# One-hot tiles with tokens in pairs: a gate matmul whose columns lie four bytes apart instead of thirty-two

## The chip, the cores and the metric

The kernel runs on one core of one Trainium2 chip. Its time is the device time of one execution in microseconds (us); three runs of the kernel before are given below. Where a part is read more closely, the numbers come from one profiled execution of it.

## The reference, cut to what matters

The program is two transformer blocks on 512 tokens of width 1024, in float32. The first block ends in a layer of product-key experts. Eight heads each choose 16 of 128 x 128 = 16384 experts for a token; an expert is a pair of rows, one of `u_tab` and one of `v_tab`, and a number `e1 * 128 + e2`.

```python
def peer(h, wq, subkeys, u_tab, v_tab):
    q = (ht @ wq).reshape(T, PEER_HEADS, 2, PEER_HALF)
    sc = jnp.einsum('thpd,hpnd->thpn', q, subkeys)
    v1, i1 = lax.top_k(sc[:, :, 0], PEER_TOPK)
    v2, i2 = lax.top_k(sc[:, :, 1], PEER_TOPK)
    ...
    best, pos = lax.top_k(cand, PEER_TOPK)
    e1 = jnp.take_along_axis(i1, pos // PEER_TOPK, axis=-1)
    e2 = jnp.take_along_axis(i2, pos % PEER_TOPK, axis=-1)
    experts = (e1 * PEER_KEYS + e2).reshape(T, PEER_HEADS * PEER_TOPK)
    gates = jax.nn.softmax(best, axis=-1).reshape(T, PEER_HEADS * PEER_TOPK)

    def block(args):
        xb, eb, gb = args
        u = jnp.take(u_tab, eb, axis=0)
        vv = jnp.take(v_tab, eb, axis=0)
        act = jax.nn.gelu(jnp.einsum('tkd,td->tk', u, xb), approximate=False)
        return jnp.einsum('tk,tkd->td', gb * act, vv)
```

## The kernel before, in words

For 448 of the 512 tokens (`ND`) the kernel does not gather expert rows. It computes the first product for all 16384 experts, 128 chunks of 128 experts (`expert_up`), takes the gelu, multiplies each value by the token's gate for that expert (zero for most), and multiplies with the second table. So it needs the gates as a dense matrix: for each token a 128 x 128 table, rows `e1`, columns `e2`. The other 64 tokens are gathered later.

The gate matrix is made in the loop `for b in range(NB)` (lines 769 to 791), 28 blocks of 16 tokens (`TB`). The partitions are the 128 choices of a token (head and rank); `e1T`, `e2T` hold the two expert halves of each choice as float16, one column a token, and `ghi`, `glo` its gate as a sum of two float16 numbers. In each block VectorE (DVE) makes four tiles of 128 x 2048 float16 numbers:

- `oa` (line 779): 1 where the index of `iot` equals `e1T`, else 0, for all 128 indices and 16 tokens; `ob` (line 780) the same for `e2T`;
- `oh` and `ol` (lines 781, 782): `ob` times `ghi`, and times `glo`.

Then TensorE multiplies, for each token, `oa` (the weights) with `oh` (line 787) and adds the product with `ol` (line 788): 32 gate matmuls a block, 128 columns each, and a weight load for each. Four tokens share a PSUM tile `gps`, which ScalarE (ACT) scales and copies to `gst` (line 789); at the end of a block `gst` is stored to DRAM as `gdr[b]` from ScalarE's queue (line 790). The tiles are laid out as `[partition, index, token]` with the 16 tokens last, so the 128 columns that one matmul reads lie 16 elements, 32 bytes, apart, for the weights as for the moving operand.

Between the blocks, `expert_up` with `on_pool=2` (line 791) spreads 22 chunks of the first expert product. A chunk is 24 matmuls of 448 columns (`part3`, lines 175, 178, 179): the weights come as float32 (`raw`, loaded from SyncE's queue) and are split by `load_w` in a rounded part `wh` (line 159) and a rest `wl` (line 162), both on GpSimd (POOL) in this stage; ScalarE takes the gelu (line 612). Outside this stage `wh` is made by ScalarE (line 161), and `wl` by VectorE or GpSimd.

The engines have queues of their own and wait for each other by semaphores; the order in each queue comes from the tile framework's scheduler. On TensorE a burst of 32 gate matmuls alternates with a chunk of 24, and at six places two bursts follow each other. `oa`, `oh` and `ol` have three buffers, `ob` one, `gst` two, `wh` and `wl` four, `raw` three, and PSUM gives eight banks to `gps` and the chunks together. After the stage come eight more chunks, and the load of `gt` from `gdr` (line 854) for the second expert product. Everything else (attention and mixer before it; experts' second product, differential attention, two feed-forward layers and a short convolution after it) isn't touched.

Of the kernel before, what the change touches and what calls it, by code (L numbers as in the profile page):

```python
# [23 lines left out]
P = 128  # L24
# [59 lines left out]
def decoder_kernel(ctx: ExitStack, tc: tile.TileContext, I, out):  # L84
# [59 lines left out]
    def after(inst, first):  # L144
        """inst is to follow first on their engine"""
        if first is not None:
            tc.add_manual_dep(inst.ins, first.ins.name, mybir.DependencyInfo(
                mybir.DependencyClass.NoSync, mybir.DependencyReason.DATA), reason="pace")
# [3 lines left out]
    def load_w(src, n=8, on_pool=0, pool=wp):  # L152
        """the two parts of a weight tile; on_pool: how many of them GpSimd makes"""
        raw = wp.tile([P, 8, P], F32, tag="raw", name="raw", bufs=3)
        wh = pool.tile([P, 8, P], F32R, tag="wh", name="wh", bufs=4)
        wl = pool.tile([P, 8, P], F32R, tag="wl", name="wl", bufs=4)
        nc.sync.dma_start(raw[:, :n], src)
        if on_pool > 1:
            G.tensor_copy(wh[:, :n], raw[:, :n])
        else:  # L160
            A.activation(wh[:, :n], raw[:, :n], AF.Copy)  # L161
        (G if on_pool else V).tensor_tensor(wl[:, :n], raw[:, :n], wh[:, :n].bitcast(F32), ALU.subtract)  # L162
        return wh, wl
# [17 lines left out]
    def linear(srcs, evac, xh=None, xl=None, N=T, n=8, on_pool=0, head=None, tail=None, between=None,  # L181
               ws=None):
        """evac(j, ps, c0, c1) takes columns c0:c1 of product j. head: column ranges of the first four products,
        done contraction step by contraction step; tail: (ranges, then) of the last four."""
        xh = xh or (lambda i: hi[:, i])
        xl = xl or (lambda i: lo[:, i])
        order = list(range(n))
        j0, j1 = 0, len(srcs)
        if head:
            j0 = len(ws or srcs[:4])  # L190
            ws = ws or [load_w(src, n, on_pool) for src in srcs[:4]]
            for c0, c1 in head:
                pss = [lin_tile()[:, :c1 - c0] for _ in ws]
                for i in order:
                    for w, ps in zip(ws, pss):
                        part3(ps, w, xh, xl, i, c0, c1, i == order[0], i == order[-1])
                    if between:
                        between(i)
                    if i >= DEFER and held and next(held[0], held) is held:
                        held.pop()  # L200
                for j, ps in enumerate(pss):
                    evac(j, ps, c0, c1)
        if tail:
            j1 -= 4
        for j in range(j0, j1):
            w = load_w(srcs[j], n, on_pool)
            ps = lin_tile()[:, :N]
            for i in order:
                part3(ps, w, xh, xl, i, 0, N, i == order[0], i == order[-1])
            evac(j, ps, 0, N)  # L210
        if tail:
            ranges, then, *pool = tail
            ws = [load_w(src, n, on_pool, *pool) for src in srcs[j1:]]
            steps = iter(())
            for c0, c1 in ranges:
                for j, w in enumerate(ws):
                    ps = lin_tile()[:, :c1 - c0]
                    for i in order:
                        part3(ps, w, xh, xl, i, c0, c1, i == order[0], i == order[-1])
                    evac(j1 + j, ps, c0, c1)  # L220
                    if j >= TDEFER:
                        next(steps, None)
                list(steps)
                steps = then(c0, c1)
            held.append(steps)
# [23 lines left out]
    def head_rstd(dst, rows, nt):  # L249
        """dst [P, nt, 16]: rstd of 64-wide heads from their rows of summed squares [16, nt * P]."""  # L250
        rw = scr.tile([P, T], F32, tag="s2k", name="rw")
# [15 lines left out]
    def head_rows(dst, r, nt):  # L267
        """dst [16, nt * P]: the rows of r [P, nt, 16]."""
        pt = ax_tile("pt")
        for t in range(nt):  # L270
            PE.transpose(pt[:16, t * P:(t + 1) * P], r[:, t], ident)
        A.activation(dst[:16, :nt * P], pt[:16, :nt * P], AF.Copy)
# [31 lines left out]
    def rstd_cols(a, c0, c1):  # L304
        """[P, 4]: rstd of each token (a column per 128 of them) from per-partition partial sums a."""
        n, nt = c1 - c0, (c1 - c0) // P
# [7 lines left out]
    def spread(r, n):  # L314
        """PSUM [P, n]: the columns of r on every partition."""
        nt = n // P
# [5 lines left out]
    def norm_apply(xt, c0, c1, a, acol, shcol, oh, ol):  # L322
        """in steps: the sums over the channels, then some channels at a time"""
        r = rstd_cols(a, c0, c1)
# [26 lines left out]

# [1 line left out]
    ws = []  # L353
# [9 lines left out]
    with tc.tile_pool(name="mix", bufs=1) as mx:  # L363
# [41 lines left out]
        def window(g):  # L405
            """the mean over the last 2 << g tokens, less the token itself"""
            cur = pch[:, g]
# [144 lines left out]
    def mod_tile(l, j, pool, cs, junk, tag):  # L552
        """columns of modulation vector tile j of layer l: ada_w products with silu(c), along the free dimension"""
        aw = pool.tile([P, D], F32, tag=tag, name="aw", bufs=3)
# [13 lines left out]
    def mod_work(pool, tiles):  # L568
        """gives step(k): runs k more of the listed (layer, tile) products; a callable in the list runs in its place"""
        cs = pool.tile([P, 1, D], F32, name="csw")  # L570
# [17 lines left out]

# [1 line left out]
    gdr = drp.tile([NB, P, P, TB], F32, name="gdr")  # L590
# [17 lines left out]
    def expert_up(c0, c1, on_pool=0):  # L608
        """gelu of the first expert product of chunks c0:c1: to DRAM below NSP, else to the end of acts"""
        def ev_u(c, ps, *_):  # L610
# [10 lines left out]
    rt = rtc.__enter__()  # L621
    iot = rt.tile([P, P, TB], F16, name="iot")
    e1T = rt.tile([P, T], F16, name="e1T")
# [5 lines left out]
    with tc.tile_pool(name="rs", bufs=1) as rs:  # L629
# [26 lines left out]
        if NG:  # L656
            for q in range(2):
# [8 lines left out]
                A.activation(h2n[:, q * T:(q + 1) * T], pn, AF.Copy)  # L666
        G.iota(iot, [[1, P], [0, TB]], base=0, channel_multiplier=0, allow_small_or_imprecise_dtypes=True)
        expert_up(0, NPRE, 1)

        # candidate pairs (a, b) of the two sorted lists that can be among the best 16: (a + 1)(b + 1) <= 16  # L670
        tvv = tv.rearrange("p t (h s) k -> p (t h) s k", s=2)
# [14 lines left out]

        # gates
        bmax = rs.tile([P, NT, 8, 1], F32, name="bmax")
# [9 lines left out]

        # expert halves of the chosen pairs
        SH = [P, NT, 16, 8]  # L700
# [68 lines left out]
    with tc.tile_pool(name="gb", bufs=2) as gb:  # L769
        for b in range(NB):  # L770
            bs = slice(b * TB, (b + 1) * TB)

            def bc(tl):
                return tl[:, bs].unsqueeze(1).to_broadcast([P, P, TB])
            oa = gb.tile([P, P, TB], F16, tag="oa", name="oa", bufs=3)
            ob = gb.tile([P, P, TB], F16, tag="ob", name="ob", bufs=1)
            oh = gb.tile([P, P, TB], F16, tag="oh", name="oh", bufs=3)
            ol = gb.tile([P, P, TB], F16, tag="ol", name="ol", bufs=3)
            V.tensor_tensor(oa, iot, bc(e1T), ALU.is_equal)
            V.tensor_tensor(ob, iot, bc(e2T), ALU.is_equal)  # L780
            V.tensor_tensor(oh, ob, bc(ghi), ALU.mult)
            V.tensor_tensor(ol, ob, bc(glo), ALU.mult)
            gst = gb.tile([P, P, TB], F32, tag="gst", name="gst")
            for t0 in range(0, TB, 4):
                ps = ax_tile("gps").rearrange("p (u n) -> p u n", u=4)
                for u in range(4):
                    PE.matmul(ps[:, u], oa[:, :, t0 + u], oh[:, :, t0 + u], start=True, stop=False)  # L787
                    last_g = PE.matmul(ps[:, u], oa[:, :, t0 + u], ol[:, :, t0 + u], start=False, stop=True)  # L788
                A.activation(gst[:, :, t0:t0 + 4].rearrange("p i t -> p t i"), ps, AF.Copy, scale=1.0 / GS)  # L789
# [7 lines left out]
    with tc.tile_pool(name="ev", bufs=1) as ev_:  # L797
# [35 lines left out]

        # row gathers and modulation, spread over the groups that also run the first expert product
        work = []
# [55 lines left out]

# [1 line left out]
    with tc.tile_pool(name="da", bufs=1) as da:  # L893
# [132 lines left out]
        with tc.tile_pool(name="at", bufs=4) as at:  # L1026
# [7 lines left out]
            def attn_out(h, aT, th):  # L1034
                """steps of the output of head h for token tiles 2 * th, 2 * th + 1"""
                W = 2 * P
# [154 lines left out]

# [1 line left out]
    mod_tiles = [(1, j) for j in range(24, 40)] + [lambda: mods_done(1, 24, 40, ((3, mod[:, 1, 32:40], "n2_1"),))]  # L1193
# [131 lines left out]
```

## Time and profile before

| | |
|---|---|
| time, median of 3 runs | 3267.92 us (3258.57, 3267.92, 3268.86) |
| span of the profiled execution, first to last instruction | 3261.2 us |
| its own time | not recorded beside the span |
| TensorE busy, share of the span | 3148.2 us, 97% |
| VectorE / ScalarE / GpSimd busy | 1846.0 / 1108.5 / 499.9 us |
| mean granted TensorE clock | 0.956 |
| one-hot operations (lines 779 to 782) | 112, median 1.22 us each |
| gate matmuls (lines 787, 788) | 896, from 401.8 us on, the last starts at 750.5 us |

How to read it: times are counted from the first instruction. A matmul's record holds its way through the array, so records of neighbours overlap; what a matmul costs is the distance from start to start. "PEclk" is the share of full clock that TensorE was granted. In a row of the list of waits stand who waited, for whom, the total in us, how often, and the longest. In a row of the timeline stand the start, the duration, the engine, the line, the operation, output and inputs.

### The profile page before, as it was taken

How to read it: one execution, taken by the hardware profiler on the slowest of the kernel's cores; microseconds unless marked ns; L12 is line 12 of the kernel's file. 1: busy time of each engine (PE TensorE's matmuls, PEld its weight loads, DVE VectorE, ACT ScalarE, POOL GpSimd, SP SyncE). 2: the span in 40 equal slices, each digit the busy share in tenths (PEclk: the TensorE clock that was granted, in tenths of full speed). 3: DMA queues.
4: the chain of work that ended last, by engine and by line, in shares of the span. 5: the costliest groups of instructions: out<-in, count | busy, mean ns of one | idle time of the engine just before them, and what ended most of it. 6: DMA issues, size and time to landing. Idle time of an engine off the chain costs nothing.

```text
span 3261.2 us, 38749 instructions
## 1 busy us (share of the span) xinstructions
PE 3148.2 (97%) x15100; PEld 2618.5 (80%) x15100; DVE 1846.0 (57%) x3378; ACT 1108.5 (34%) x1611; POOL 499.9 (15%) x438
## 2 busy tenths in 40 slices
PE   8999799999999999999999999999999999999999
PEld 6688677778899888888888877655888888898887
DVE  6678943422775666666666574287654446653333
ACT  4433233334233232232232353276422233332221
POOL 1133422113000222222222020000000000000000
PEclk9999877679999999999999999999999999999999
DMA  4222333336775776666666332000364434533332
GB/s 141 65 73 92 115 125 138 120 133 216 230 238 154 234 237 227 221 230 222 227 227 221 120 129 68 26 1 27 102 203 142 130 116 130 161 129 92 91 101 78
DMA packets 132071, 467.24 MB, mean 143 GB/s; under 512 B 14896, under 2 KB 25312, under 8 KB 127920
## 3 DMA queue, kind: packets, MB, share of 16 engines
q1 hardware_dynamic: 79200, 269.56, 26.3%
q0 software_dynamic: 42752, 156.59, 14.6%
q10 hardware_dynamic: 9936, 38.63, 3.0%
q8 instruction: 118, 1.93, 0.3%
q14 instruction: 65, 0.53, 0.0%
HBM read 419.86 MB, written 40.63 MB: 141 GB/s over the span
## 4 chain that ended last, share of the span: by engine, by line
PE 59%; issue 18%; DMA 11%; DVE 8%; POOL 2%; ACT 2%; POOLq 0%; DVEq 0%; ACTq 0%
PE mm L175 14%; PE mm L179 14%; PE mm L178 14%; DMA gu<-in_peer_ur,idx 4%; DMA gu<-in_peer_vr,idx 4%; PE gps L787 3%; PE gps L788 3%; PE sp L1086 2%; PE po L1044 1%; DMA aw<-in_ada_w 1%; DMA gt<-gdr 1%; DVE wl L162 1%; POOL gu L820 1%; PE mm L1010 1%; PE mm L1012 1%
## 5 line engine op out<-in xcount | busy, mean ns | idle before, releaser
L179 PE MATMUL mm<-hi,wl 128*128 128x512 f32 (+2 forms) x2496 | 930.7, 373 | 41.9 <-DVE wl L162 39.9
L175 PE MATMUL mm<-hi,wh 128*128 128x512 f32 (+2 forms) x2496 | 937.9, 376 | 13.3 <-ACT wh L161 8.2
L161 ACT ACTIVATE wh<-raw 128x1024 fp32r<-128x1024 f32 (+1 forms) x468 | 491.4, 1052 | 1338.4 <-PE mm L178 871.9
L178 PE MATMUL mm<-lo,wh 128*128 128x512 f32 (+2 forms) x2496 | 928.9, 372 | 0.0
L162 DVE TENSOR_TENSOR wl<-raw,wh 128x1024 fp32r<-128x1024 f32 (+1 forms) x425 | 515.0, 1214 | 281.6 <-ACT wh L161 275.7
L179 PEld LDWEIGHTS mm<-hi,wl 128*128 128x128 f32 x2496 | 483.5, 194 | 117.2 <-DVE wl L162 49.6
L175 PEld LDWEIGHTS mm<-hi,wh 128*128 128x128 f32 x2496 | 485.8, 195 | 84.1 <-ACT wh L161 11.3
L178 PEld LDWEIGHTS mm<-lo,wh 128*128 128x128 f32 x2496 | 484.6, 194 | 64.1 <-issue 0.8
L178 PE MATMUL mm<-pl,wh 128*128 128x448 f32 (+3 forms) x1436 | 523.4, 364 | 5.1 <-DVE pl L871 5.1
L179 PE MATMUL mm<-ph,wl 128*128 128x448 f32 (+3 forms) x1436 | 523.3, 364 | 0.8 <-DVE wl L162 0.8
L175 PE MATMUL mm<-ph,wh 128*128 128x448 f32 (+3 forms) x1436 | 523.3, 364 | 0.5 <-ACT ph L870 0.5
L178 PEld LDWEIGHTS mm<-pl,wh 128*128 128x128 f32 x1436 | 270.5, 188 | 33.8 <-DVE pl L871 5.8
L179 PEld LDWEIGHTS mm<-ph,wl 128*128 128x128 f32 x1436 | 270.6, 188 | 30.1 <-DVE wl L162 1.9
L175 PEld LDWEIGHTS mm<-ph,wh 128*128 128x128 f32 x1436 | 270.5, 188 | 29.0 <-ACT ph L870 0.9
L162 POOL TENSOR_TENSOR wl<-raw,wh 128x1024 fp32r<-128x1024 f32 x65 | 159.3, 2455 | 225.1 <-ACT wh L161 201.5
L787 PE MATMUL gps<-oh,oa 128*128 128x128 f16 x448 | 188.8, 423 | 0.0
L788 PE MATMUL gps<-ol,oa 128*128 128x128 f16 x448 | 188.0, 422 | 0.0
L789 ACT ACTIVATE gst<-gps 128x512 f32<-128x512 f32 x112 | 122.1, 1092 | 106.4 <-PE gps L788 104.9
L866 DVE TENSOR_TENSOR act<-act,gt 128x448 f32<-128x448 f32 x128 | 79.8, 634 | 104.1 <-DMA gt<-gdr 98.6
L347 DVE SCALAR_TENSOR_TENSOR x<-mm,mod,x 128x512 f32<-128x512 f32 (+1 forms) x76 | 50.5, 666 | 148.4 <-PE mm L179 148.2
L555 POOL DMA_DIRECT2D aw<-in_ada_w x96 | 52.3, 546 | 519.1 <-DVE mod L556 330.9
L870 ACT ACTIVATE ph<-act 128x448 fp32r<-128x448 f32 x128 | 72.7, 576 | 151.3 <-DVE act L866 150.8
(350 smaller groups left out, 3341.6 us busy)
## 6 DMA issues: line engine op xcount, KB each, us to landing
raw<-in_peer_u SPq DMA_DIRECT2D x128, 512.0 KB, 4.0
raw<-in_peer_v SPq DMA_DIRECT2D x128, 512.0 KB, 3.7
aw<-in_ada_w POOLq DMA_DIRECT2D x96, 512.0 KB, 5.0
raw<-in_w_gu SPq DMA_DIRECT2D x88, 512.0 KB, 3.7
gdr<-gst ACTq DMA_DIRECT2D x28, 1024.0 KB, 3.9
gt<-gdr POOLq DMA_DIRECT2D x16, 1792.0 KB, 11.7
raw<-in_w_dn SPq DMA_DIRECT2D x32, 448.0 KB, 3.4
raw<-in_sc_in SPq DMA_DIRECT2D x24, 512.0 KB, 3.7
```

The source lines that it names most:

```text
L161: A.activation(wh[:, :n], raw[:, :n], AF.Copy)
L162: (G if on_pool else V).tensor_tensor(wl[:, :n], raw[:, :n], wh[:, :n].bitcast(F32), ALU.subtract)
L175: mm = PE.matmul(ps, wh[:, i], xh(i)[:, c0:c1], start=first, stop=False)
L178: PE.matmul(ps, wh[:, i], xl(i)[:, c0:c1], start=False, stop=False)
L179: PE.matmul(ps, wl[:, i], xh(i)[:, c0:c1], start=False, stop=last)
L555: nc.gpsimd.dma_start(aw, I["ada_w"][l, j])
L787: PE.matmul(ps[:, u], oa[:, :, t0 + u], oh[:, :, t0 + u], start=True, stop=False)
L788: last_g = PE.matmul(ps[:, u], oa[:, :, t0 + u], ol[:, :, t0 + u], start=False, stop=True)
L789: A.activation(gst[:, :, t0:t0 + 4].rearrange("p i t -> p t i"), ps, AF.Copy, scale=1.0 / GS)
L866: V.tensor_tensor(at.rearrange("p (b t) -> p b t", t=TB), at.rearrange("p (b t) -> p b t", t=TB), gt[:, :, c], ALU.mult)
L870: A.activation(ph, at, AF.Copy)
L1086: PE.matmul(sps[e][:, c0:c1], q2[pr, qi, ts], k2[pr, qi, c0:c1], start=True, stop=True)
```

## The change

The tiles `oa`, `ob`, `oh` and `ol` become `[partition, token pair, index, token of the pair]`: 8 pairs, 128 indices, 2 tokens. The columns of one matmul then lie 2 elements, four bytes, apart. `iot` holds each index twice instead of 16 times and is read again for each pair (a step of 0); the vectors `e1T`, `e2T`, `ghi`, `glo` are read two tokens at a time, and each two are repeated over the 128 indices. Sizes of the tiles, count of operations and of matmuls, and the numbers computed are the same. (The diff also drops comments, left out here.)

```diff
-    iot = rt.tile([P, P, TB], F16, name="iot")
+    iot = rt.tile([P, P, 2], F16, name="iot")
...
-        G.iota(iot, [[1, P], [0, TB]], base=0, channel_multiplier=0, allow_small_or_imprecise_dtypes=True)
+        G.iota(iot, [[1, P], [0, 2]], base=0, channel_multiplier=0, allow_small_or_imprecise_dtypes=True)
...
+            PAIRS = [P, TB // 2, P, 2]
+
             def bc(tl):
-                return tl[:, bs].unsqueeze(1).to_broadcast([P, P, TB])
-            oa = gb.tile([P, P, TB], F16, tag="oa", name="oa", bufs=3)
-            ob = gb.tile([P, P, TB], F16, tag="ob", name="ob", bufs=1)
-            oh = gb.tile([P, P, TB], F16, tag="oh", name="oh", bufs=3)
-            ol = gb.tile([P, P, TB], F16, tag="ol", name="ol", bufs=3)
-            V.tensor_tensor(oa, iot, bc(e1T), ALU.is_equal)
-            V.tensor_tensor(ob, iot, bc(e2T), ALU.is_equal)
+                return tl[:, bs].rearrange("p (a u) -> p a u", u=2).unsqueeze(2).to_broadcast(PAIRS)
+            oa = gb.tile(PAIRS, F16, tag="oa", name="oa", bufs=3)
+            ob = gb.tile(PAIRS, F16, tag="ob", name="ob", bufs=1)
+            oh = gb.tile(PAIRS, F16, tag="oh", name="oh", bufs=3)
+            ol = gb.tile(PAIRS, F16, tag="ol", name="ol", bufs=3)
+            io = iot.unsqueeze(1).to_broadcast(PAIRS)
+            V.tensor_tensor(oa, io, bc(e1T), ALU.is_equal)
+            V.tensor_tensor(ob, io, bc(e2T), ALU.is_equal)
             V.tensor_tensor(oh, ob, bc(ghi), ALU.mult)
             V.tensor_tensor(ol, ob, bc(glo), ALU.mult)
...
                 for u in range(4):
-                    PE.matmul(ps[:, u], oa[:, :, t0 + u], oh[:, :, t0 + u], start=True, stop=False)
-                    last_g = PE.matmul(ps[:, u], oa[:, :, t0 + u], ol[:, :, t0 + u], start=False, stop=True)
+                    at = (slice(None), (t0 + u) // 2, slice(None), u % 2)
+                    PE.matmul(ps[:, u], oa[at], oh[at], start=True, stop=False)
+                    last_g = PE.matmul(ps[:, u], oa[at], ol[at], start=False, stop=True)
```

On TensorE, VectorE, ScalarE and SyncE the instructions stand in the same order as before, row for row. On GpSimd one instruction has another size, the index pattern of line 667, made before the expert layer's first product:

```order
 L247 TENSOR_TENSOR r_1336<-rp,mhalf 128x2
 L602 DMA fold<-in_fold 128x64
-L667 IOTA iot 128x2048
+L667 IOTA iot 128x256
 L631 DMA skT<-in_subkeys 128x2048
 L247 TENSOR_TENSOR r_1551<-rp,mhalf 128x2
```

Nothing moved there; `iot` is written with 256 elements a partition in place of 2048.

## The prediction

> **What bounds the kernel now.** I read the page first: its span, the two rows of section 2 for TensorE, and the groups of the gate matmuls.
>
> ```profile
> span 3261.2 us, 38749 instructions
> PE   8999799999999999999999999999999999999999
> PEclk9999877679999999999999999999999999999999
> L787 PE MATMUL gps<-oh,oa 128*128 128x128 f16 x448 | 188.8, 423 | 0.0
> L788 PE MATMUL gps<-ol,oa 128*128 128x128 f16 x448 | 188.0, 422 | 0.0
> L789 ACT ACTIVATE gst<-gps 128x512 f32<-128x512 f32 x112 | 122.1, 1092 | 106.4 <-PE gps L788 104.9
> ```
>
> TensorE is busy from end to end, so what it saves shows at the end unless another engine is late. Its clock is low in slices 5 to 9, and the gate matmuls run there. The table of windows gives that stage from the first gate matmul to the last, the stretch after it, and then the gate matmuls alone (the last two rows) in a stretch at full clock and one at half clock.
>
> ```profile
> core 0: us, PE busy (x) PEld busy (x) DVE busy (x) ACT busy (x) POOL busy (x), PEclk, DMA share, GB/s
> 401.76:750.53 348.77, 348.77 (x1402) 253.04 (x1401) 130.36 (x107) 133.07 (x133) 69.91 (x39) 0.71 0.34 126
> 769.00:810.00 41.00, 40.33 (x195) 35.98 (x194) 18.35 (x23) 19.39 (x25) 12.13 (x9) 1.00 0.81 267
> ...
> core 0: us, PE busy (x), PEclk, DMA share, GB/s
> 452.90:456.40 3.50, 3.50 (x15) 1.00 0.17 61
> 456.60:467.90 11.30, 11.30 (x49) 0.50 0.38 139
> ```
>
> In the stage TensorE never stops; VectorE (DVE), ScalarE (ACT) and GpSimd (POOL) are busy for 130, 133 and 70 us of 349. The list of waits says on whom they wait:
>
> ```profile
> POOL wh L159 <- PE mm L178: 222.5, 18, 19.0
> DVE oh L781 <- PE gps L787: 105.0, 12, 9.3
> ACT gst L789 <- PE gps L788: 104.0, 108, 2.3
> DVE oa L779 <- PE gps L788: 74.4, 12, 8.8
> ```
>
> All of them wait for TensorE. The important reading is in the last two window rows: a gate matmul takes 3.50 / 15 = 0.233 us at full clock and 11.30 / 49 = 0.231 us at half clock. What costs the same at both clocks isn't limited by the array; what is left is the reading of the two operands, whose 128 columns lie 32 bytes apart. The 896 matmuls at 0.235 us (a burst of 32 from 438.81 to 446.34 us) are 211 us of the stage. The other 138 us are 21 chunks of the first expert product, 504 matmuls of 448 columns, 0.274 us each on average. The timeline shows why these too are slow:
>
> ```profile
> 434.32 0.57 PE L175 MATMUL mm<-hi,wh 128*128 128x448 f32 x1
> 434.69 0.57 PE L178 MATMUL mm<-lo,wh 128*128 128x448 f32 x1
> ...
> 436.34 0.36 PE L175 MATMUL mm<-hi,wh 128*128 128x448 f32 x1
> 436.54 0.37 PE L178 MATMUL mm<-lo,wh 128*128 128x448 f32 x1
> ...
> 438.81 0.45 PE L787 MATMUL gps<-oh,oa 128*128 128x128 f16 x1
> ...
> 446.34 0.74 PE L175 MATMUL mm<-hi,wh 128*128 128x448 f32 x1
> ```
>
> After a gate burst they start 0.37 us apart (half clock), some 4 us later 0.20 us apart. So a gate burst, busy by the record, doesn't hold the clock up.
>
> **What the change costs and saves.** No instruction is added, removed or moved on TensorE, VectorE, ScalarE or SyncE. GpSimd's index pattern becomes an eighth as large; it is made at 174 us, long before its first use at 393 us, and counts as nothing. What changes is how long the 896 gate matmuls (with their weight loads) and the 112 one-hot operations take.
>
> *Gate matmul at a step of four bytes.* No row has two-byte columns at this step, so I bound it. Below: 448-column matmuls at full clock, whose four-byte columns also lie four bytes apart, start 0.20 us apart, so 128 columns are 0.058 us. Above: 128-column matmuls in plain float32, each with weights of its own:
>
> ```profile
> 283.86 1.16 PE L649 MATMUL pss<-skT,qt 128*128 128x128 f32 x8
> 284.86 0.27 PE L665 MATMUL pn<-ident,tmp 128*128 128x128 f32 x1
> ```
>
> Eight in 1.00 us are 0.125 us each. I take 0.07, near the lower end: the step is that of the 448-column rows, and plain float32 costs twice as much a column there. TensorE then needs 896 x 0.07 = 63 us, and 504 x 0.203 = 102 us for the expert chunks if the clock stays up: 165 us instead of 349. Alone, it would finish at 402 + 165 = 567 us.
>
> [...]
>
> *What is late next.* VectorE and GpSimd. Their timelines where both are busy, and GpSimd alone:
>
> ```profile
> 393.30 1.23 DVE L779 TENSOR_TENSOR oa<-iot,e1T 128x2048 f16<-128x2048 f16 x1
> 394.44 1.22 DVE L780 TENSOR_TENSOR ob<-iot,e2T 128x2048 f16<-128x2048 f16 x1
> ...
> 396.72 1.22 DVE L781 TENSOR_TENSOR oh<-ob,ghi 128x2048 f16<-128x2048 f16 x1
> 397.85 2.06 DVE L782 TENSOR_TENSOR ol<-ob,glo 128x2048 f16<-128x2048 f16 x1
> 399.84 3.42 DVE L779 TENSOR_TENSOR oa<-iot,e1T 128x2048 f16<-128x2048 f16 x1
> 403.17 2.06 DVE L780 TENSOR_TENSOR ob<-iot,e2T 128x2048 f16<-128x2048 f16 x1
> ...
> 469.56 1.22 DVE L780 TENSOR_TENSOR ob<-iot,e2T 128x2048 f16<-128x2048 f16 x1
> 470.82 1.23 DVE L781 TENSOR_TENSOR oh<-ob,ghi 128x2048 f16<-128x2048 f16 x1
> ...
> 398.92 3.25 POOL L162 TENSOR_TENSOR wl<-raw,wh 128x1024 fp32r<-128x1024 f32 x1
> 402.12 2.04 POOL L159 CAST wh<-raw 128x1024 fp32r<-128x1024 f32 x1
> 473.98 1.04 POOL L159 CAST wh<-raw 128x1024 fp32r<-128x1024 f32 x1 [17.64 <-PE mm L178]
> 475.10 2.38 POOL L162 TENSOR_TENSOR wl<-raw,wh 128x1024 fp32r<-128x1024 f32 x1
> ```
>
> A one-hot operation alone takes 1.14 us from start to start (393.30 to 394.44). The one that starts at 399.84 while GpSimd subtracts until 402.17 takes 3.42 us: it waits until GpSimd is done and then needs its 1.1 us. GpSimd's 2.38 us become 3.25 in the same way. The two engines take turns, so their times add. Today that is hidden, as both idle most of the stage. From 393.3 us on there are 112 VectorE operations, 28 x (4 x 1.14 + 0.12) = 131 us (0.12: where `oh` directly follows the `ob` that it reads, it starts 470.82 - 469.56 = 1.26 us after it, not 1.14), and 20 chunks on GpSimd at 1.04 + 2.38 = 3.42 us, 68 us. Together 199 us: the last operands are ready at 592 us, later than TensorE's 567, so this pair ends the stage. The last 32 gate matmuls take 2 us more: 595 us instead of 750.5, 155 us less. Where the pair stands still for a moment, or TensorE falls to half clock while it waits for operands, some of that is lost; I allow 8 us (one 0.3 us gap for each block), which leaves **147 us**.
>
> ScalarE needs its 133 us and stays under 199. The stage's 44 MB (349 us at 126 GB/s) in 193 us would be 228 GB/s, less than the 267 of the stretch at 769 us. What follows (eight more chunks, then the load of the gates from DRAM) hangs on the end of the stage in the same order and moves with it; the clock comes back there some us sooner, which I don't count.
>
> *One-hot operations in the new layout.* All of their operands still have neighbouring elements last, but the gate and index vectors now come in runs of two elements instead of sixteen. The shortest runs that the trace has at two bytes are eight:
>
> ```profile
> 372.06 0.42 DVE L734 TENSOR_TENSOR prd<-msk,li 128x512 f16<-128x512 f16 x1
> 372.39 0.29 DVE L729 TENSOR_SCALAR msk<-bb 128x512 f16<-128x512 f16 x1
> ```
>
> 512 elements take 0.33 us from start to start and 2048 take 1.14, so the 1536 more cost 0.81 us: 0.53 ns an element, with runs of eight as with runs of sixteen, and some 0.06 us are fixed. So I take 1.14 us unchanged. Bounds: no gain below, since no two-byte row of this engine with two operands is quicker per element; above, half that rate, as if the two elements of a run were handled one by one: 2048 x 1.06 ns + 0.06 = 2.2 us.
>
> [...] No run here shows runs of two.
>
> **Sum.** The page is one execution with a span of 3261.2 us; the three runs are 3258.57, 3267.92 and 3268.86 us, so some 7 us lie around the span, or the execution was a quicker one. Against the median: 3268 - 147 = **3121 us**. A difference under 0.3% (10 us, the spread of those runs) can't be told from none.
>
> **Rivals.**
> - *TensorE stays the bound (0.17).* Either a gate matmul costs 0.125 us, 112 + 102 = 214 us, the stage ends at 616, 134 us less: 3134 us. (The pair is overtaken from (592 - 402 - 102) / 896 = 0.098 us on.) Or the clock doesn't come back: 504 x 0.373 + 896 x 0.107 (0.373 x 128 / 448) = 284 us, end at 686, 3203 us. For it: half clock follows each burst today. Against it: denser matmuls elsewhere hold 1.00. [...]
> - *VectorE falls to half its rate (0.10).* 28 x (4 x 2.20 + 0.12) + 68 = 318 us, end at 711 + 2, 37 us less: 3231 us. For it: no row has such short runs. Against it: runs of eight cost nothing over sixteen.
> - *The gate matmul doesn't get faster (0.04).* If any gap between columns, not the 32 bytes, costs 0.235 us, nothing changes: 3268 us. Four-byte columns at the same step speak against it.
> - *Slower (0.03).* If each run of two costs VectorE three steps, where it now costs one of 1.06 ns (two elements at 0.53), an operation is 1024 x 3 x 1.06 = 3.2 us + 0.06, the pair needs 28 x 13.2 + 68 = 438 us, and the stage ends at 833: 83 us more, 3351 us. This decides from (750 - 2 - 393 - 68) / 112 = 2.56 us an operation on.
>
> **Numbers.** The forecast has 0.66. Its own range is 3102 (the pair overlaps a little, as from 396.72 to 408.48 us where 12.5 us of work took 11.8, and the later matmuls find a full clock) to 3140. With the first half of the first rival the range goes to 3162. Faster by over 0.3%: 0.66 + 0.17 + 0.10 = 0.93; same 0.04; slower 0.03.
>
> **What would show it.** Gate matmuls start 0.06 to 0.1 us apart. The stage takes 190 to 205 us. VectorE has next to no idle time in it, and its operations still have a least time of 1.22 us with more of them stretched to 2 to 3.4. TensorE now waits for `ol` or `oh` from VectorE, for the first time. The clock of the stage rises over 0.9. The windows from the stage's end on look as before. I am wrong if the gate matmuls stay above 0.1 us, the one-hot operations get longer when nothing contends, or VectorE idles while TensorE waits.

## The result

The changed kernel takes 3111.19 us (median of 4 runs, 3109.35 to 3115.48), the kernel before 3266.22 us in the same comparison. The ratio is 0.9532, with a 95% interval from 0.9517 to 0.9547: 155 us, 4.7%, less. In the page of the kernel after, the span and the two rows of TensorE:

```profile
span 3109.8 us, 38748 instructions
PE   8899788899999999999999999999999999999999
PEclk9999889999999999999999999999999999999999
```

Of the dip of the clock in slices 5 to 9, two slices at 8 tenths are left. The table of windows shows the gate stage, from its first gate matmul to the last, and then one burst of 32 gate matmuls alone (columns as in the prediction):

```profile
402.04:595.46 193.42, 166.57 (x1401) 153.20 (x1401) 181.32 (x107) 114.46 (x131) 91.78 (x39) 0.93 0.62 223
...
478.00:485.00 7.00, 2.01 (x32) 1.00 0.46 184
```

The stage takes 193.4 us where it took 348.8; that is 155.4 us less, all of the 155 us between the medians. TensorE now is busy for 167 us of it, VectorE for 181. The burst alone lasts from 480.78 to 482.60, 0.057 us a gate matmul instead of 0.235. Behind a long wait it is slower:

```profile
480.78 0.23 PE L792 MATMUL gps<-oh,oa 128*128 128x128 f16 x1
...
482.60 0.45 PE L175 MATMUL mm<-hi,wh 128*128 128x448 f32 x1
...
570.63 0.29 PE L792 MATMUL gps<-oh,oa 128*128 128x128 f16 x1 [4.48 <-DVE oa L783]
571.76 0.27 PE L793 MATMUL gps<-ol,oa 128*128 128x128 f16 x1 [0.84 <-DVE ol L786]
571.83 0.31 PE L792 MATMUL gps<-oh,oa 128*128 128x128 f16 x1
571.93 0.31 PE L793 MATMUL gps<-ol,oa 128*128 128x128 f16 x1
572.04 0.31 PE L792 MATMUL gps<-oh,oa 128*128 128x128 f16 x1
```

From 571.83 to 574.92 us the granted clock is 0.50, and the matmuls start 0.107 us apart. Five of the 28 bursts are of this kind, wholly or in part, each behind a wait of 3.1 to 4.9 us: some 114 of the 896 gate matmuls. The list of waits of this stage has turned round:

```profile
POOL wh L159 <- PE mm L178: 73.0, 18, 11.7
PE gps L792 <- DVE oa L783: 9.7, 3, 4.5
PE gps L793 <- DVE ol L786: 8.8, 8, 3.1
PE gps L792 <- DVE oh L785: 8.4, 2, 4.9
DVE oa L783 <- PE gps L793: 0.5, 1, 0.5
```

Before, VectorE waited 179 us for gate matmuls. Now it waits 0.5 us, and TensorE waits 27 us for VectorE (all three tiles). What VectorE and GpSimd (POOL) do in the middle of the stage, and how the stage ends, is in the timeline:

```profile
426.01 3.32 DVE L785 TENSOR_TENSOR oh<-ob,ghi 128x2048 f16<-128x2048 f16 x1
429.26 1.21 DVE L786 TENSOR_TENSOR ol<-ob,glo 128x2048 f16<-128x2048 f16 x1
430.51 2.11 DVE L784 TENSOR_TENSOR ob<-iot,e2T 128x2048 f16<-128x2048 f16 x1
432.65 3.27 DVE L785 TENSOR_TENSOR oh<-ob,ghi 128x2048 f16<-128x2048 f16 x1
435.84 1.21 DVE L786 TENSOR_TENSOR ol<-ob,glo 128x2048 f16<-128x2048 f16 x1
...
430.50 1.04 POOL L159 CAST wh<-raw 128x1024 fp32r<-128x1024 f32 x1 [2.24 <-PE mm L178]
431.62 3.23 POOL L162 TENSOR_TENSOR wl<-raw,wh 128x1024 fp32r<-128x1024 f32 x1
...
584.88 1.22 DVE L786 TENSOR_TENSOR ol<-ob,glo 128x2048 f16<-128x2048 f16 x1
...
593.65 0.23 PE L792 MATMUL gps<-oh,oa 128*128 128x128 f16 x1
```

An `ob` that meets GpSimd's rounding, and an `oh` that meets its subtraction, take 2.1 and 3.3 us instead of 1.2, and GpSimd's own subtraction takes 3.2 instead of 2.4: they take turns. VectorE works through from 393.6 to 586.1 us. The last burst starts only at 593.65, since TensorE is then behind: GpSimd has finished its last chunk of the stage at 568 us, and from there VectorE is quicker (4.86 us a block) than TensorE with a burst and a chunk (1.82 + 4.89). The burst at half clock before these blocks adds 1.5 us to that.

### The profile page after: what moved, and what is told of

Same layout as the page of the kernel before. It is cut to its first block, busy times and chain, and to the rows that moved or that the text cites. A ratio compares the mean times of both kernels' runs of the same rounds, so it can differ in the third digit from the quotient of the medians.

```text
span 3109.8 us, 38748 instructions
## 1 busy us (share of the span) xinstructions
PE 2969.9 (96%) x15100; PEld 2519.1 (81%) x15100; DVE 1897.2 (61%) x3378; ACT 1091.9 (35%) x1611; POOL 521.0 (17%) x438
## 4 chain that ended last, share of the span: by engine, by line
PE 52%; issue 18%; DVE 14%; DMA 11%; POOL 3%; ACT 2%; DVEq 0%; POOLq 0%; ACTq 0%; SPq 0%
PE mm L179 14%; PE mm L175 14%; PE mm L178 13%; DMA gu<-in_peer_ur,idx 4%; DMA gu<-in_peer_vr,idx 4%; PE sp L1091 2%; DVE ob L784 2%; DVE oh L785 1%; DMA aw<-in_ada_w 1%; PE po L1049 1%; DVE ol L786 1%; DVE oa L783 1%; DMA gt<-gdr 1%; DVE wl L162 1%; PE mm L1015 1%
## 5 line engine op out<-in xcount | busy, mean ns | idle before, releaser
L179 PE MATMUL mm<-hi,wl 128*128 128x512 f32 (+2 forms) x2496 | 918.4, 368 | 40.0 <-DVE wl L162 37.1
L175 PE MATMUL mm<-hi,wh 128*128 128x512 f32 (+2 forms) x2496 | 922.1, 370 | 13.3 <-ACT wh L161 8.1
L178 PE MATMUL mm<-lo,wh 128*128 128x512 f32 (+2 forms) x2496 | 916.0, 367 | 0.0
L179 PEld LDWEIGHTS mm<-hi,wl 128*128 128x128 f32 x2496 | 474.5, 190 | 112.9 <-DVE wl L162 46.0
L175 PEld LDWEIGHTS mm<-hi,wh 128*128 128x128 f32 x2496 | 475.6, 191 | 80.1 <-ACT wh L161 11.2
L178 PEld LDWEIGHTS mm<-lo,wh 128*128 128x128 f32 x2496 | 475.5, 191 | 62.4 <-issue 0.8
L162 POOL TENSOR_TENSOR wl<-raw,wh 128x1024 fp32r<-128x1024 f32 x65 | 174.0, 2679 | 196.4 <-ACT wh L161 172.9
L829 DVE CUSTOM_DVE_ANT_0 gjk<-gu,h2n 128x1024 f16<-128x1024 f32 x64 | 78.3, 1223 | 71.4 <-DMA gu<-in_peer_ur,idx 71.1
L345 DVE TENSOR_TENSOR x<-x,mm 128x448 f32<-128x448 f32 (+2 forms) x132 | 80.2, 608 | 67.1 <-PE mm L179 66.9
L794 ACT ACTIVATE gst<-gps 128x512 f32<-128x512 f32 x112 | 106.1, 1105 | 28.6 <-PE gps L793 25.8
```

The source lines that it names most:

```text
L175: mm = PE.matmul(ps, wh[:, i], xh(i)[:, c0:c1], start=first, stop=False)
L178: PE.matmul(ps, wh[:, i], xl(i)[:, c0:c1], start=False, stop=False)
L179: PE.matmul(ps, wl[:, i], xh(i)[:, c0:c1], start=False, stop=last)
L345: V.tensor_tensor(x[:, j, c0:c1], x[:, j, c0:c1], ps, ALU.add)
L829: dve_gated(V.tensor_tensor_reduce(gjk, gu, h2n, 1.0, 0.0, ALU.mult, ALU.add, dot[:, s:s + 1]))
```

## The experiments

**Which operand, and which distance.** The layouts were varied by two numbers, `GA` for the weights `oa` and `GM` for `ob`, `oh` and `ol`: so many tokens lie side by side, and the columns are twice as many bytes apart. The changed kernel is `GA = GM = 2`, the one before 16.

```diff
-            PAIRS = [P, TB // 2, P, 2]
+            GA, GM = 2, 16        # w4_m32; 16, 2: w32_m4; 4, 4: step8; 8, 8: step16; 1, 1: step2
+            def sh(g):
+                return [P, TB // g, P, g]
...
-                    at = (slice(None), (t0 + u) // 2, slice(None), u % 2)
+                    wa, ma = ((slice(None), (t0 + u) // g, slice(None), (t0 + u) % g) for g in (GA, GM))
-                    PE.matmul(ps[:, u], oa[at], oh[at], start=True, stop=False)
+                    PE.matmul(ps[:, u], oa[wa], oh[ma], start=True, stop=False)
```

*Weights 4 bytes apart, moving operand 32:*

> Weights in pairs (4 bytes apart), moving operand as before (32 bytes apart). Theory A, the moving operand's read sets the 0.235 us: a gate matmul stays at 0.23 us from start to start and the time stays near 3266 us. Theory B, the weights' read sets it: 0.06 to 0.1 us and about 3111 us. Theory C, each of the two reads alone takes 0.23 us, side by side: 0.23 us here and in the opposite mix too. Theory D, the two reads follow each other and half of the cost is each one's: about 0.14 us here and there, stage 896 x 0.14 + 504 x 0.21 = 231 us, time about 3150 us.

*Weights 32 bytes apart, moving operand 4:*

> Weights as before (32 bytes apart), moving operand in pairs (4 bytes apart). Theory A (moving operand): 0.06 to 0.12 us a gate matmul, time about 3111 to 3135 us. Theory B (weights): 0.23 us and 3266 us. Theory C (each alone): 0.23 us and 3266 us. Theory D (half each): 0.14 us and about 3150 us.

Timeline and weight loads (least, median and longest time in ns) of the first, then of the second:

```profile
479.77 0.41 PE L796 MATMUL gps<-oh,oa 128*128 128x128 f16 x1
480.00 0.41 PE L797 MATMUL gps<-ol,oa 128*128 128x128 f16 x1
480.24 0.41 PE L796 MATMUL gps<-oh,oa 128*128 128x128 f16 x1
...
L796 PEld LDWEIGHTS <-oa x448: 96/128/152, 404.2 to 741.2; 128*128 128x128 f16 x150
```

```profile
484.62 0.23 PE L797 MATMUL gps<-ol,oa 128*128 128x128 f16 x1
484.68 0.23 PE L796 MATMUL gps<-oh,oa 128*128 128x128 f16 x1
484.75 0.23 PE L797 MATMUL gps<-ol,oa 128*128 128x128 f16 x1
...
L796 PEld LDWEIGHTS <-oa x448: 141/148/164, 401.2 to 595.8; 128*128 128x128 f16 x150
```

With the weights in pairs a gate matmul stays at 0.23 us (three starts in 0.47 us) and the time at 3257.1 us, one run, against 3267.6 for the kernel before on that chip. With the moving operand in pairs it is 0.065 us and 3107.7 us. So the moving operand's reads made nearly the whole price (theory A). The weights' load is longer at 32 bytes, 148 ns against 97 in the changed kernel, but runs beside the matmuls; 0.065 - 0.057 = 0.008 us a gate matmul is all that it costs.

*Both operands 8, and both 16 bytes apart:*

> Four tokens side by side: columns 8 bytes apart, for both operands. [...] If any step above 4 bytes pays in full: 0.23 us, 3266 us.

> Eight tokens side by side: columns 16 bytes apart, for both operands, one column a 16-byte line. If a read pays for each line: 0.23 us a gate matmul as at 32 bytes, 3266 us. If the price goes with the distance: 0.118 us, stage 106 + 104 = 210 us, from 402 to 612, about 3128 us. If 16 bytes is still free: 0.057 us and 3111 us.

Timeline of a burst and the window of most of the stage, at 8 and then at 16 bytes:

```profile
479.83 0.30 PE L795 MATMUL gps<-ol,oa 128*128 128x128 f16 x1
479.95 0.30 PE L794 MATMUL gps<-oh,oa 128*128 128x128 f16 x1
480.07 0.30 PE L795 MATMUL gps<-ol,oa 128*128 128x128 f16 x1
...
420.00:600.00 180.00, 180.00 (x1206) 169.38 (x1204) 139.15 (x97) 101.87 (x114) 73.50 (x35) 1.00 0.59 212
```

```profile
484.37 0.42 PE L795 MATMUL gps<-ol,oa 128*128 128x128 f16 x1
484.60 0.41 PE L794 MATMUL gps<-oh,oa 128*128 128x128 f16 x1
484.83 0.41 PE L795 MATMUL gps<-ol,oa 128*128 128x128 f16 x1
...
420.00:700.00 280.00, 280.00 (x1164) 204.49 (x1163) 113.98 (x97) 108.12 (x110) 65.40 (x36) 0.72 0.36 131
```

0.117 us (bursts of 32 in 3.7 us) and 3138.1 us at 8 bytes, 0.233 us and 3244.8 us at 16, one run each. A price that goes with the distance, 0.235 us at 32 bytes, would be 0.059 and 0.118 us; a full price for any step above 4 bytes, 0.23 us for both: neither fits the two. What fits the steps from 4 to 32 bytes is a price for each 16-byte line, each stretch of 16 bytes, that the moving operand touches, worked out from these times alone: 128 lines cost 0.233 us at 16 and 0.235 at 32 bytes, 1.82 ns a line; 64 lines cost 0.117, again 1.82; 32 lines, the step of four bytes, would cost 0.058, and 0.057 was measured. The 448-column rows of the prediction can't tell whether that is the lines or the array, as they too hold four columns a line (112 lines x 1.82 = 0.204 us). The columns next to each other, below, can: 16 lines would cost 0.029 us, and it is still 0.055. So below 32 lines something else sets the time, and of the steps tried four bytes is the largest that is nearly free at two bytes an element (0.057 us against 0.055). The weights moved with the moving operand in these two runs; that their step costs little was seen only beside a moving operand at 4 bytes (0.008 us). At 8 bytes TensorE is busy throughout at full clock: there it is the bound again, as the first rival had it.

**Columns next to each other.**

> One token after the other: columns next to each other (2 bytes apart), so that the index vectors are read with a step of 0 innermost. If VectorE then falls to one element a step (the prediction's rival of half rate): the operations with such a vector take 2.2 us, the turns come to 28 x (4 x 2.2 + 0.12) + 68 = 318 us, stage end at 712 to 720, about 3228 us, while the gate matmul stays at 0.057 us. If VectorE keeps its rate: 1.22 us and 3111 us.

Groups of the one-hot operations, three gate matmuls at full clock, and the longest row of TensorE's waits in the stage:

```profile
L785 DVE TENSOR_TENSOR oa<-iot,e1T x28: 2275/2293/4483, 389.5 to 688.9; 128x2048 f16<-128x2048 f16 x28
L788 DVE TENSOR_TENSOR ol<-ob,glo x28: 2277/2286/4474, 401.3 to 706.6; 128x2048 f16<-128x2048 f16 x28
...
580.37 0.22 PE L794 MATMUL gps<-oh,oa 128*128 128x128 f16 x1
580.42 0.22 PE L795 MATMUL gps<-ol,oa 128*128 128x128 f16 x1
580.48 0.22 PE L794 MATMUL gps<-oh,oa 128*128 128x128 f16 x1
...
PE gps L794 <- DVE oh L787: 93.9, 21, 8.7
```

All four operations fall to 2.29 us, `oh` and `ol` too, though only one of their inputs is read with a step of 0. The gate matmul takes 0.055 us at full clock, and the last starts at 712.7 us, where the sum of turns puts it (712 to 720); the time is 3221.7 us, one run. This is the prediction's second rival come true in another layout, within 10 us of its price.

**What ends the stage.** Two kernels take GpSimd's work away, by the last argument of the stage's `expert_up`; the third does it in the kernel before.

```diff
-            expert_up(NPRE + NMID + b * NDUR // NB, NPRE + NMID + (b + 1) * NDUR // NB, 2)
+            expert_up(NPRE + NMID + b * NDUR // NB, NPRE + NMID + (b + 1) * NDUR // NB, 0)   # pool1: 1
```

> The changed kernel, with the weights of the 22 expert chunks of the gate stage split on ScalarE (rounded part) and VectorE (rest) instead of GpSimd. Theory, the stage ends when VectorE and GpSimd, who take turns, have done their work: VectorE then has 131 + 22 x 1.14 = 156 us and no partner, TensorE needs 896 x 0.057 + 504 x 0.204 = 154 us plus waits, so the stage ends near 565 instead of 595 us and the time is about 3082 us. Rival, TensorE's own order and waits end the stage: no change, 3111 us, or slower where TensorE waits for the rest that now stands behind one-hot operations.

> The changed kernel, with the rounded part of those weights on ScalarE and the rest still on GpSimd. Theory of turns: 131 + 20 x 2.38 = 179 us instead of 192, the stage ends about 13 us sooner, about 3098 us. Rival (TensorE's own waits): 3111 us.

> The kernel before, with those weights split on ScalarE and VectorE instead of GpSimd. Theory: there the two engines idle behind TensorE, so taking GpSimd's work away saves nothing: 3266 us within 10 us. Rival, that the turns of VectorE and GpSimd already cost time before: 20 us or more faster.

Measured: 3089.26 us (ratio to the kernel before 0.9465, 95% 0.9434 to 0.9496), 3099.73 us (0.9494, 0.9473 to 0.9515), and 3263.49 us (0.9994, 0.998 to 1.0008). The windows of the stage, in the first and in the third:

```profile
398.19:574.93 176.74, 163.82 (x1402) 149.36 (x1401) 144.47 (x125) 132.80 (x152) 2.38 (x1) 0.94 0.67 250
```

```profile
394.70:746.70 352.00, 351.39 (x1402) 254.01 (x1401) 146.13 (x125) 150.94 (x153) 2.39 (x1) 0.71 0.34 127
```

Without GpSimd's share the stage of the changed kernel takes 177 us, of which TensorE is busy for 164. The last gate matmul starts at 574.9 us, 10 us later than the 565 that I expected. The longest of TensorE's waits for gate matmuls is now for ScalarE, which does a part of the splitting:

```profile
PE gps L792 <- ACT gst L794: 8.3, 3, 3.4
```

With only the rounding away (1.04 of the 3.42 us a chunk) the last gate matmul starts at 582 us, 13 us sooner, as expected. In the kernel before the same edit moves the splitting to VectorE (23 us) and ScalarE (21 us) and changes nothing: TensorE is busy for 351.4 of 352 us.

**The other way round: less work for TensorE.**

```diff
-                    PE.matmul(ps[:, u], oa[at], oh[at], start=True, stop=False)
-                    last_g = PE.matmul(ps[:, u], oa[at], ol[at], start=False, stop=True)
+                    last_g = PE.matmul(ps[:, u], oa[at], oh[at], start=True, stop=True)
```

> The changed kernel without the second gate matmul of each token (line 793): the low part of the gates is left out of the result, and VectorE still makes its tile. 448 matmuls at 0.057 us, 25.5 us of TensorE, are gone. Theory, VectorE and GpSimd end the stage: it ends at 586 to 592 us instead of 595, time 3105 to 3111 us. Rival, TensorE ends it: about 25 us less, 3086 us.

> The same omission in the kernel before: 448 matmuls at 0.235 us, 105 us of TensorE, are gone. Theory, TensorE bounds the stage there: at least 105 us less, up to 115 us with a little more of the clock, 3150 to 3160 us. Rival, another engine or a wait is close behind: clearly less than 105 us gained.

Waits of the stage, in the changed kernel and in the one before, each with this omission:

```profile
PE gps L792 <- DVE oh L785: 44.8, 11, 7.3
```

```profile
DVE oa L779 <- PE gps L787: 69.7, 20, 6.3
```

In the changed kernel 25.5 us less of TensorE's work bring 3107.9 us, one run; the changed kernel's median on that chip is 3114.0. The wait for `oh` grows instead, and the last gate matmul starts at 587 us. In the kernel before 105 us less bring 3161.8 us, one run, 104 less than the 3265.5 of its runs there and 2 us above the range that I expected; the last gate matmul starts at 642.8 instead of 750.5.

**The better version once more**, beside the changed kernel in the same rounds:

> The changed kernel once more, on the chip and in the rounds of after_pool0_again: about 3111 us.

> The changed kernel with the stage's weights split on ScalarE and VectorE, beside the changed kernel on one chip. Theory of turns: 15 to 30 us faster than the changed kernel, about 3089 us. Rival (the first measurement, 3082 to 3099 us, was scatter): within 10 us of it.

3114.03 us (ratio 0.952, 0.9498 to 0.9543; five runs from 3096.54 to 3115.30) and 3083.76 us (0.9445, 0.9429 to 0.9461; five from 3077.57 to 3087.76). The intervals don't meet: with the weights of the stage split on ScalarE and VectorE the kernel is 30 us quicker than the changed one, and 182 us quicker than the one before (3265.51 in these rounds).

## Why the prediction was right

It said 3121 us (3102 to 3162); the median is 3111. Step by step:

- *The reads, not the array, set the gate matmul's time.* Right; the equal times at both clocks (0.233 and 0.231 us) were the row to read. The mixed layouts add that it was the moving operand (0.23 us with it at 32 bytes, 0.065 at 4), but for 0.008 us.
- *0.07 us at four bytes.* Measured 0.057 at full clock, the lower bound, and 0.107 for the some 114 behind long waits: 782 x 0.057 + 114 x 0.107 = 57 us, where I had 63. The 6 us hardly reach the end, as TensorE isn't the bound of most of the stage; `after_half` shows what such a saving is worth.
- *The turns of VectorE and GpSimd end the stage.* Right, and shown from three sides: taking GpSimd's work away makes it shorter, slower one-hot operations make it longer by the predicted sum, and 25.5 us less work on TensorE bring its end only 8 us forward (587 instead of 595.5). The sum was 199 us; 393.63 to 586.10 are 192.5. That the two overlap a little at each handover is enough for the 7 us: in the timeline above an `ob`, an `oh` and a chunk take 430.51 to 435.84, 5.33 us, 0.49 less than their times alone (1.26 + 1.14 + 3.42), and there are 20 chunks. The prediction had seen this from 396.72 to 408.48 us, put it into its range and left it out of its sum.
- *The end.* 595 us was forecast for the last gate matmul before the allowance, and it is 595.5. That is luck, as two errors cancel: the operands are ready 6 us sooner, and TensorE is 9.4 us behind them where I had put 2. I had taken the two sums as wholes; near the end GpSimd has nothing left, and TensorE is the slower one for the last blocks.
- *The allowance of 8 us for gaps* is the term that was too large: within the stage VectorE's operations follow each other with hardly a gap. They waited 0.5 us for TensorE in all, so of TensorE's half clock behind its waits only the last such burst, 1.5 us, can have reached the end. Behind the stage the kernel loses 3.7 us: from the last gate matmul to the end are 2510.7 us before (3261.2 - 750.5) and 2514.3 after (3109.8 - 595.5). The granted clock is 0.99 in both stretches; what makes the difference, no run shows.
- *One-hot operations unchanged by runs of two.* Right: those that meet no work of GpSimd take 1.21 to 1.23 us.
- *The clock comes back.* 0.93 in the stage, and most chunks take 4.89 us (0.204 us a matmul). It still falls to 0.50 behind long waits (3.1 to 4.9 us), as the prediction had feared. The clock rival, 3203 us, is out at this step.

## What to carry to other kernels

When a matmul takes the same time at half and at full clock (here 0.231 and 0.233 us), look at how far apart the columns of its moving operand lie: count the 16-byte lines that it touches, here 1.82 ns each, against the time that it takes with its columns next to each other, here 0.055 us. Before summing such a gain, add up what the other engines need in that stage, engines that take turns as one: here TensorE's busy time in the stage fell by 182 us (348.8 to 166.6); 155 of them reached the end, and the other 27 became waits. The engine that is late next is where the next edit belongs: moving GpSimd's share away did nothing before the change and 30 us after it.

## What I had not expected of the hardware

- A gate matmul at 8 bytes takes 0.117 us, twice the 0.057 at four, and at 16 bytes 0.233, twice that again, but at 32 no more (0.235).
- The layout whose gate matmuls take 0.117 us (8 bytes) held the granted clock at 1.00 through 420 to 600 us; the one at 0.233 us (16 bytes) was granted 0.72 from 420 to 700 us, near the 0.71 of the stage before the change, though TensorE never stood still by its records (280.00 of 280.00 us busy).
- With a step of 0 innermost in one of two inputs, VectorE's one-hot operations on two-byte elements took 2.29 us instead of 1.22.
